# A feed-forward's second projection as 2x2 blocks in seven products

## The chip, the cores and the metric

The kernel runs on one core of a Trainium2 chip. The metric is the device time of one execution in microseconds; 2852.32 is the median of three runs (2851.64 to 2853.88). The engines are named as the profile names them: PE is TensorE (PEld its weight loads), DVE VectorE, ACT ScalarE, POOL GpSimd, SP SyncE.

## What is computed

One transformer block of two layers (attention mixers, then a feed-forward with a convolution) and a second block with a plain gated feed-forward, a mixer and a feed-forward again, on 512 tokens of width 1024 in float32: seven stages m0, f0, m1, f1, s0, m2, s1, of which four (f0, f1, s0, s1) are feed-forwards. Only these change:

```python
def conv_ffn(h, w_up, conv_w, conv_b, w_down):          # f0, f1
    u = h @ w_up                                        # 1024 -> 2 x 2816
    u = lax.conv_general_dilated(u, conv_w[:, None, :], ...) + conv_b   # over 3 tokens, per channel
    gate, up = jnp.split(u, 2, axis=-1)
    return (jax.nn.gelu(gate, approximate=True) * up) @ w_down          # 2816 -> 1024

def _swiglu(x, w_gate, w_up, w_down):                   # s0, s1
    return (jax.nn.silu(x @ w_gate) * (x @ w_up)) @ w_down
```

What comes out is normed, scaled by a gain and added to the residual x; the next stage begins with a norm of x.

## The kernel before

Every float32 operand of a matmul is split in two: hi, a rounded copy that ScalarE makes, and lo, the rest, a subtraction on VectorE. A product is three matmuls (hi·hi, hi·lo, lo·hi, `mm3`, lines 220 to 225).

`Weights` (line 30) is the planner. SyncE loads chunks of up to 1 MB into two raw buffers (`_load`, line 89). A chunk holds units of 1024 columns per partition, and `_split` (line 103) writes a unit's hi and lo into one of four slots; the last unit's rest also issues the load of the chunk after the next (line 122). `get` takes the next unit, `done` frees a slot and splits ahead as far as slots go. `lend` adds slots for a few units. Every engine runs its instructions in the order in which the program writes them, so a split that waits for a load holds what is behind it on ScalarE.

A feed-forward (`ffn`, line 603) runs in two parts of 11 k-tiles (a k-tile: 128 of the 2816 inner channels). For each pair of k-tiles `gemm_T` computes two gate and two up tiles (128 channels x 512 tokens, 24 matmuls each); `post_g` and `post_u` turn them into the product g, and `split2` (line 227) writes it into `gh`, `gl`. Behind the 11 k-tiles follows the second projection with `out_part` (line 520): output half h (512 columns), four token tiles of 128, stationary `gh[:, k, tokens]`, moving the weight unit. The first part's result goes into `part`; the second part's (`out_last`, line 553) is added, squared on ScalarE for the norm, and multiplied by the gain (half 0 on VectorE, half 1 on GpSimd). The last four units run token tile by token tile, and `finish` (line 575) makes a token tile's new x and, through `pre_norm` (line 329), its normed row hn, which `turn` (line 371) transposes on TensorE and `evacuate` splits for the next stage. From there on rests of weights are made on GpSimd (`W.lo`), ahead for the next stage.

Of the kernel before, what the change touches and what calls it, by code (L numbers as in the profile page):

```python
# [16 lines left out]
T = 512  # L17
# [11 lines left out]

class Weights:  # L30
# [6 lines left out]
    def __init__(self, nc, pool):  # L37
# [6 lines left out]
        self.units = []  # L44
        self.loaded = 0
# [25 lines left out]
    def add(self, srcs, a, b, unit_slices):  # L71
        c = len(self.chunks)
        self.chunks.append((srcs, a, b))
        for n, (a0, a1, b0, b1) in enumerate(unit_slices):
            self.units.append((c, a0, a1, b0, b1, n == len(unit_slices) - 1))
# [27 lines left out]
    def _split(self):  # L103
        u = self.split
        c, a0, a1, b0, b1, last = self.units[u]
        _, a, b = self.chunks[c]
        if c >= self.loaded:
            self.flush()
        raw = self.raw[c % self.NRAW][:, :a * b].rearrange("p (a b) -> p a b", a=a)[:, a0:a1, b0:b1]
# [3 lines left out]
        self.late.append((lo, raw, hi, c + self.NRAW if last else 0))  # L113
# [4 lines left out]
    def flush(self):  # L118

        for lo, raw, hi, nxt in self.late:  # L120
            self.lo.tensor_sub(lo, raw, hi.bitcast(F32))  # L121
            self._load(nxt)
        self.late = []

    def ahead(self, keep=1):

        self.flush()
        while self.split < len(self.units):
# [8 lines left out]
    def view(self, u):  # L137
        _, a0, a1, b0, b1, _ = self.units[u]
        n = (a1 - a0) * (b1 - b0)
        return tuple(t[:, :n].rearrange("p (a b) -> p a b", a=a1 - a0) for t in self.where[u])  # L140
# [33 lines left out]
class Net:  # L174
# [418 lines left out]
    def reg_ffn(self, wg, wg0, wu, wu0, wd):  # L593
        W = self.W
        for k0, nk in ((0, 11), (11, 11)):
            for j in range(k0, k0 + nk, 2):
                m = min(2, k0 + nk - j)
                W.cols(wg, wg0 + j * 128, m * 128)
                W.cols(wu, wu0 + j * 128, m * 128)
            for h in range(2):  # L600
                W.rows(wd, k0, nk, h * 512, 512)

    def ffn(self, conv, half, last, gpost, gpre_next):
# [3 lines left out]
        with ExitStack() as st:  # L607
            P = st.enter_context(self.tc.tile_pool(name="ffn", bufs=1))
            gh = P.tile([128, 11, T], F32R, name="gh")
            gl = P.tile([128, 11, T], F32R, name="gl")  # L610
            part = P.tile([128, 4, D], F32, name="part")
            tmp = ExitStack()
            Q = tmp.enter_context(self.tc.tile_pool(name="ffntmp", bufs=1))
            cg = [Q.tile([128, T], F32, name=f"cg{i}") for i in range(3)]
            gg = [Q.tile([128, T], F32, name=f"gg{i}") for i in range(2)]
            if conv is not None:
                cu = [Q.tile([128, T], F32, name=f"cu{i}") for i in range(3)]
                cw = Q.tile([128, 2 * NFT, 4], F32, name="cw")
                nc.gpsimd.dma_start(cw, conv)

# [15 lines left out]
            def post_u(j, jj):  # L636
                def f(ps):
                    g = gg[j % 2]
                    if conv is not None:
# [4 lines left out]
                    self.split2(gh[:, jj], gl[:, jj], g)  # L644
# [5 lines left out]
            for p in range(2):  # L650
                k0 = p * 11
                for jj in range(0, 11, 2):
                    m = min(2, 11 - jj)
                    posts = [post_g(k0 + jj + e) for e in range(m)] + [post_u(k0 + jj + e, jj + e) for e in range(m)]
# [6 lines left out]
                if p == 0:  # L661
                    for h in range(2):
                        def post0(i, ps):
                            if i % 2:
                                nc.vector.tensor_copy(part[:, i, h * 512:h * 512 + 512], ps)
                            else:
                                nc.scalar.activation(part[:, i, h * 512:h * 512 + 512], ps, AF.Copy)
                        self.out_part((gh, gl), 11, post0)
                else:
# [1084 lines left out]
```

## Time and profile before

| | us |
|---|---|
| median of the runs | 2852.32 |
| profiled execution: its own time | 2851.37 |
| profiled execution: span from first to last instruction | 2849.4 |
| TensorE busy | 2790.2 |
| VectorE busy | 1397.4 |
| ScalarE busy | 1102.0 |
| GpSimd busy | 365.3 |

Busy time of TensorE counts pipelined records that overlap, so its share says that it hardly ever waits, not that it runs at its peak; what one matmul costs is the distance from start to start.

### The profile page before, as it was taken

How to read it: one execution, taken by the hardware profiler on the slowest of the kernel's cores; microseconds unless marked ns; L12 is line 12 of the kernel's file. 1: busy time of each engine (PE TensorE's matmuls, PEld its weight loads, DVE VectorE, ACT ScalarE, POOL GpSimd, SP SyncE). 2: the span in 40 equal slices, each digit the busy share in tenths (PEclk: the TensorE clock that was granted, in tenths of full speed). 3: DMA queues.
4: the chain of work that ended last, by engine and by line, in shares of the span. 5: the costliest groups of instructions: out<-in, count | busy, mean ns of one | idle time of the engine just before them, and what ended most of it. 6: DMA issues, size and time to landing. Idle time of an engine off the chain costs nothing.

```text
span 2849.4 us, 34641 instructions
## 1 busy us (share of the span) xinstructions
PE 2790.2 (98%) x14196; PEld 2282.4 (80%) x14196; DVE 1397.4 (49%) x2126; ACT 1102.0 (39%) x1886; POOL 365.3 (13%) x285
## 2 busy tenths in 40 slices
PE   8999999999999999999999999999999999999998
PEld 7778688888878787788888888888777978888887
DVE  4666645535555666455535453233653343533334
ACT  3444634423444456444334332223343322432232
POOL 5221100100122221000101110000522000000000
PEclk9999999999999999999999999999999999999999
DMA  4211132333322111233332323323421223322332
GB/s 148 74 57 34 34 130 86 105 115 108 111 71 91 60 38 45 82 119 95 108 103 91 110 89 100 100 81 118 140 74 53 72 78 97 111 94 92 104 97 73
DMA packets 234318, 255.45 MB, mean 90 GB/s; under 512 B 33072, under 2 KB 193184, under 8 KB 233776
## 3 DMA queue, kind: packets, MB, share of 16 engines
q1 hardware_dynamic: 228016, 233.53, 25.7%
q0 software_dynamic: 4992, 16.94, 1.9%
q8 instruction: 111, 1.82, 0.3%
q10 hardware_dynamic: 1152, 2.77, 0.3%
q14 instruction: 47, 0.39, 0.0%
HBM read 248.60 MB, written 5.53 MB: 89 GB/s over the span
## 4 chain that ended last, share of the span: by engine, by line
PE 90%; DVE 5%; ACT 3%; issue 1%; DMA 0%; DVEq 0%; ACTq 0%; POOL 0%; POOLq 0%
PE PS L223 26%; PE PS L225 25%; PE PS L224 25%; PE PS L422 2%; DVE x L585 2%; PE PS L1124 1%; PE PS L1110 1%; PE PS L1080 1%; PE PS L425 1%; PE PS L460 1%; DVE hn L339 1%; PE PS L1220 1%; PE PS L1192 1%; PE PS L380 1%; PE PS L1511 1%
## 5 line engine op out<-in xcount | busy, mean ns | idle before, releaser
L121 DVE TENSOR_TENSOR wlo<-wraw,whi 128x1024 fp32r<-128x1024 f32 (+3 forms) x366 | 440.3, 1208 | 726.5 <-ACT whi L112 726.4
L223 PE MATMUL PS<-Hh,whi 128*128 128x512 f32 x1952 | 776.1, 398 | 4.1 <-DVE oBl L232 2.8
L225 PE MATMUL PS<-Hh,wlo 128*128 128x512 f32 x1952 | 761.0, 390 | 0.9 <-DVE wlo L121 0.9
L224 PE MATMUL PS<-Hl,whi 128*128 128x512 f32 x1952 | 760.6, 390 | 0.0
L112 ACT ACTIVATE whi<-wraw 128x1024 fp32r<-128x1024 f32 (+2 forms) x432 | 436.9, 1016 | 340.0 <-PE PS L225 279.5
L223 PEld LDWEIGHTS PS<-Hh,whi 128*128 128x128 f32 x1952 | 366.5, 188 | 88.3 <-issue 8.7
L225 PEld LDWEIGHTS PS<-Hh,wlo 128*128 128x128 f32 x1952 | 366.4, 188 | 79.2 <-DVE wlo L121 1.5
L224 PEld LDWEIGHTS PS<-Hl,whi 128*128 128x128 f32 x1952 | 367.0, 188 | 70.5
L121 POOL TENSOR_TENSOR wlo<-wraw,whi 128x1024 fp32r<-128x1024 f32 (+1 forms) x66 | 162.8, 2467 | 1268.1 <-ACT whi L112 1268.1
L223 PE MATMUL PS<-whi,gh 128*128 128x512 f32 x624 | 242.8, 389 | 0.0
L224 PE MATMUL PS<-wlo,gh 128*128 128x512 f32 x624 | 242.7, 389 | 0.0
L225 PE MATMUL PS<-whi,gl 128*128 128x512 f32 x624 | 242.7, 389 | 0.0
L231 ACT ACTIVATE gh<-gg 128x512 fp32r<-128x512 f32 x88 | 55.7, 632 | 327.2 <-DVE gg L643 178.9
L223 PEld LDWEIGHTS PS<-whi,gh 128*128 128x128 f32 x624 | 117.3, 188 | 24.3
L225 PEld LDWEIGHTS PS<-whi,gl 128*128 128x128 f32 x624 | 117.1, 188 | 24.4
L224 PEld LDWEIGHTS PS<-wlo,gh 128*128 128x128 f32 x624 | 117.1, 188 | 24.4
L641 POOL TENSOR_TENSOR gg<-cg,cu 128x512 f32<-128x512 f32 x44 | 56.7, 1289 | 549.4 <-DVE cu L624 549.4
L232 DVE TENSOR_TENSOR gl<-gg,gh 128x512 fp32r<-128x512 f32 x88 | 60.9, 693 | 125.6 <-ACT gh L231 125.6
L223 PE MATMUL PS<-whi,Hh 128*128 128x512 f32 (+2 forms) x320 | 118.2, 369 | 1.9 <-ACT whi L112 1.6
L224 PE MATMUL PS<-wlo,Hh 128*128 128x512 f32 (+2 forms) x320 | 116.7, 365 | 0.5 <-DVE wlo L121 0.5
L225 PE MATMUL PS<-whi,Hl 128*128 128x512 f32 (+2 forms) x320 | 116.5, 364 | 0.0
L1091 DVE TENSOR_REDUCE small<-PS 128x2 f32<-128x256 f32 (+3 forms) x64 | 52.7, 824 | 72.0 <-PE PS L1082 61.2
(355 smaller groups left out, 3966.0 us busy)
## 6 DMA issues: line engine op xcount, KB each, us to landing
wraw<-in_w_in_dram SPq DMA_DIRECT2D x56, 1024.0 KB, 5.0
wraw<-in_w_up_dram SPq DMA_DIRECT2D x40, 1024.0 KB, 5.1
wraw<-in_ffn_w_gate_dram SPq DMA_DIRECT2D x20, 1024.0 KB, 5.2
wraw<-in_ffn_w_up_dram SPq DMA_DIRECT2D x20, 1024.0 KB, 5.3
wraw<-in_w_down_dram SPq DMA_DIRECT2D x16, 1024.0 KB, 5.0
wraw<-in_ffn_w_down_dram SPq DMA_DIRECT2D x16, 1024.0 KB, 5.0
wraw<-in_w_out_dram SPq DMA_DIRECT2D x12, 1024.0 KB, 4.9
wraw<-in_w_down_dram SPq DMA_DIRECT2D x8, 768.0 KB, 4.3
```

Source lines behind the costliest of these rows:

```text
L112: self.nc.scalar.activation(hi, raw, AF.Copy)
L121: self.lo.tensor_sub(lo, raw, hi.bitcast(F32))
L223: mm(out, lh, rh, start=start, stop=False)
L224: mm(out, lh, rl, start=False, stop=False)
L225: mm(out, ll, rh, start=False, stop=stop)
L231: nc.scalar.activation(hi, src, AF.Copy)
L232: nc.vector.tensor_sub(lo, src, hi.bitcast(F32))
L339: nc.vector.scalar_tensor_tensor(hn, self.x[:, i], r, self.gpre, op0=OP.mult, op1=OP.mult)
L422: self.nc.tensor.matmul(ps[:, sl], ww[:, k], self.Hh[:, k, sl], start=k == 0 and ww is w[0], stop=False)
L585: nc.vector.scalar_tensor_tensor(x, f, r, x, op0=OP.mult, op1=OP.add)
L641: nc.gpsimd.tensor_mul(g, cg[j % 3], cu[j % 3])
L1091: nc.vector.reduce_max(m, S2, axis=AX.X, negate=True)
```

## The change

The second projection of each part becomes a product of 2x2 blocks. Even and odd k-tiles of the part are the two blocks of the inner dimension, tokens 0 to 255 and 256 to 511 the two of the rows, the output halves the two of the columns. Seven products of sums of blocks, added into the four output blocks with signs, replace the eight plain ones. A feed-forward has three parts (6, 8 and 8 k-tiles, so P = 3, 4, 4 pairs).

`post_u` makes the sums of activation blocks with four VectorE operations for every pair of k-tiles and splits seven operands of 256 tokens (`Ah`, `Al`). `Weights.quad` lists the weight units in the order of the products: the raw buffers hold two blocks (x and y), a third (z) is loaded by SyncE into free rows, and the sums are made in place, by accumulating transfers from GpSimd's queue, each issued when the unit that it overwrites has been split. `down` runs the seven products ("steps"), keeps three pairs of PSUM banks of which two are accumulated into more than once, and adds each output into `part` with its sign. In the last part (`fin`) it also squares, multiplies by the gain (both halves on VectorE), queues `finish`, and splits the next stage's units; three operands' places are lent as slots. `out_part` and `out_last` stay for the other stages. The core of the diff:

```diff
@@ -72,7 +78,45 @@
+    def quad(self, w, k0, P):
+        v = w.rearrange("(k p) n -> p k n", p=128)
+        block = lambda o, h: v[:, k0 + o:k0 + 2 * P:2, h * 512:h * 512 + 512]
+        b12, b21, b22 = block(0, 1), block(1, 0), block(1, 1)
+        c, q = len(self.chunks), Quad()
+        self.chunks += [([(0, 128, b)], P, 512) for b in (b22, block(0, 0))]
+        q.block, q.P = b21, P
+        part = [slice(i, min(i + 2, P)) for i in range(0, P, 2)]
+        y = lambda i: self.raw_of(c)[:, part[i]]
+        x = lambda i: self.raw_of(c + 1)[:, part[i]]
+        z = lambda i: q.room[i][:, :part[i].stop - part[i].start]
+        plus = lambda t, b: lambda i: self.nc.gpsimd.dma_start(t(i), b[:, part[i]], accum_op=OP.add)
+        load = lambda c: lambda i: self._load(c) if i == len(part) - 1 else None
+        for src, after in ((x, plus(x, b12)), (x, plus(x, b22)), (y, plus(y, b12)), (z, None), (x, plus(x, b21)),
+                           (y, load(c + 2)), (x, load(c + 3))):
+            for i, s in enumerate(part):
+                self.units.append((c + 1, lambda i=i, src=src: src(i), s.stop - s.start, 512,
+                                   [lambda i=i, f=after: f(i)] if after else []))
+        self.quads.append(q)
+    def open_quad(self, room):
+        q = self.quads.pop(0)
+        q.room = room
+        for i in range(0, q.P, 2):
+            m = min(2, q.P - i)
+            self.nc.sync.dma_start(room[i // 2][:, :m], q.block[:, i:i + m])
+        return q.P
...
     def flush(self):
-        for lo, raw, hi, nxt in self.late:
+        late, self.late = self.late, []
+        for lo, raw, hi, after in late:
             self.lo.tensor_sub(lo, raw, hi.bitcast(F32))
-            self._load(nxt)
-        self.late = []
-    def ahead(self, keep=1):
+            for f in after:
+                f()
+    def ahead(self, keep=1, upto=1 << 30):
...
     def reg_ffn(self, wg, wg0, wu, wu0, wd):
         W = self.W
-        for k0, nk in ((0, 11), (11, 11)):
+        for k0, nk in self.PARTS:
             for j in range(k0, k0 + nk, 2):
-                m = min(2, k0 + nk - j)
-                W.cols(wg, wg0 + j * 128, m * 128)
-                W.cols(wu, wu0 + j * 128, m * 128)
-            for h in range(2):
-                W.rows(wd, k0, nk, h * 512, 512)
+                W.cols(wg, wg0 + j * 128, 256)
+                W.cols(wu, wu0 + j * 128, 256)
+            W.quad(wd, k0, nk // 2)
+    PARTS = ((0, 6), (6, 8), (14, 8))
+    def down(self, Ah, Al, room, part, first, fin=None):
+        nc, W = self.nc, self.W
+        u0 = W.taken
+        if fin:
+            self.normed = 0
+            W.lend([tuple(t[:, op].rearrange("p m t -> p (m t)") for t in (Ah, Al)) for op in (0, 3, 6)], 10)
+        P = W.open_quad(room)
+        nu = (P + 1) // 2
+        a, b, c = [[self.bank(), self.bank()] for _ in range(3)]
+        steps = ((0, a, False, 0, 0, 1, True, False), (3, b, False, 1, 1, -1, True, False), (6, b, True, 0, 1, -1, True, False),
+                 (1, c, False, 0, 0, 1, False, True), (4, a, True, 0, 1, -1, False, True), (5, a, True, 1, 1, -1, False, True),
+                 (2, a, True, 1, 0, 1, True, True))
+        for n, (op, banks, on, row, h, sign, new, end) in enumerate(steps):
+            ws = [W.get() for _ in range(nu)]
+            if fin:
+                if n == 2:
+                    self.table(SQRT_SET)
+                W.ahead(0, u0 + nu * (n + (3 if n == 3 else 2)))
+                if n == 5:
+                    W.defer, W.lo = True, nc.gpsimd
+                    W.ahead(0)
+            else:
+                W.ahead(0)
+            for e in range(2):
+                i, ps = 2 * row + e, banks[e]
+                tok = slice(e * 128, e * 128 + 128)
+                for m in range(P):
+                    lhs = Ah[:, op, m, tok], Al[:, op, m, tok]
+                    w = ws[m // 2]
+                    for x, (l, r) in enumerate(((0, 0), (0, 1), (1, 0))):
+                        nc.tensor.matmul(ps, lhs[l], w[r][:, m % 2], start=not on and m + x == 0, stop=m == P - 1 and x == 2,
+                                         skip_group_check=on)
+                    if fin and n == 6 and e == 1 and m == P // 2 - 1:
+                        self.bi += 2
+                        self.turn(1)
+                        self.evacuate()
+                if e == 1:
+                    W.free_only(nu)
+                f = part[:, i, h * 512:h * 512 + 512]
+                if new and first:
+                    if e:
+                        nc.vector.tensor_scalar(f, ps, float(sign), None, op0=OP.mult)
+                    else:
+                        nc.scalar.activation(f, ps, AF.Copy, scale=float(sign))
+                elif sign > 0:
+                    nc.vector.tensor_add(f, ps, f)
+                else:
+                    nc.vector.tensor_sub(f, f, ps)
+                if fin:
+                    if n == 6 and e == 0:
+                        self.turn(0)
+                    if end:
+                        fin(i, h, c[e] if n in (4, 5) else ps)
+                    self.pump()
+                    self.evacuate()
+                    W.flush()
+        if fin:
+            self.pump()
+            W.ahead(0)
+            W.flush()
+            W.defer, W.lo = False, nc.vector
+            W.give_back()
...
-            gh = P.tile([128, 11, T], F32R, name="gh")
...
+            Ah = P.tile([128, 7, 4, 256], F32R, name="Ah")
+            Al = P.tile([128, 7, 4, 256], F32R, name="Al")
...
+            S = [h.rearrange("p (s t) -> p s t", s=4) for h in self.hn]
...
-                    self.split2(gh[:, jj], gl[:, jj], g)
+                    m, s = jj // 2, S[jj // 2 % 2]
+                    (g11, g21), (g12, g22) = [[t[:, h * 256:h * 256 + 256] for h in range(2)] for t in gg]
+                    if jj % 2 == 0:
+                        late.append(lambda: self.split2(Ah[:, 0, m], Al[:, 0, m], g11))
+                    else:
+                        nc.vector.tensor_sub(s[:, 0], g22, g21)
+                        nc.vector.scalar_tensor_tensor(s[:, 1], s[:, 0], -1.0, g11, op0=OP.mult, op1=OP.subtract)
+                        nc.vector.tensor_sub(s[:, 2], g11, g21)
+                        nc.vector.scalar_tensor_tensor(s[:, 3], g12, -1.0, s[:, 1], op0=OP.mult, op1=OP.subtract)
+                        late.append(lambda: self.split2(Ah[:, 1:3, m], Al[:, 1:3, m], g.rearrange("p (h t) -> p h t", h=2)))
+                        late.append(lambda: self.split2(Ah[:, 3:7, m], Al[:, 3:7, m], s))
...
+                run_late()
+                e = (k0 + nk - 2) % 3
+                room = [tm[:, 2 * i:2 * i + 2] for i in ((e + 2) % 3, e, (e + 1) % 3, 3)]
+                def fin(i, h, sq):
+                    f = part[:, i, h * 512:h * 512 + 512]
+                    nc.scalar.activation(sq, f, AF.Square, accum_out=sst[:, h * 4 + i:h * 4 + i + 1])
+                    nc.vector.tensor_mul(f, f, self.gpost[:, h * 512:h * 512 + 512])
+                    if h == (i < 2):
+                        self.side.append(self.finish(i, part[:, i, :512], part[:, i, 512:], sst[:, i:i + 1],
+                                                     sst[:, 4 + i:5 + i], half, last))
+                self.down(Ah, Al, room, part, p == 0, fin if k0 + nk == NFT else None)
+            while self.side:
+                self.pump()
```

## Rows read from the trace of the kernel before

**Rows 1.** The page of the whole span: its head, busy share per engine, TensorE's clock

```profile
span 2849.4 us, 34641 instructions
...
PE 2790.2 (98%) x14196; PEld 2282.4 (80%) x14196; DVE 1397.4 (49%) x2126; ACT 1102.0 (39%) x1886; POOL 365.3 (13%) x285
...
PEclk9999999999999999999999999999999999999999
```

**Rows 2.** Timeline of TensorE, first and last of 117: start us, length us, instruction

```profile
559.71 0.39 PE L225 MATMUL PS<-Hh,wlo 128*128 128x512 f32 x1
...
586.01 0.39 PE L224 MATMUL PS<-Hl,whi 128*128 128x512 f32 x1
```

**Rows 3.** Groups of TensorE in 559.9 to 586.05 us; one of three alike

```profile
L223 PE MATMUL PS<-Hh,whi 128*128 128x512 f32 x39 | 15.2, 389 | 0.0
```

**Rows 4.** Groups, whole span: second projections' first term (count, busy us, mean ns, idle)

```profile
L223 PE MATMUL PS<-whi,gh 128*128 128x512 f32 x624 | 242.8, 389 | 0.0
...
L223 PE MATMUL PS<-mhi,gh 128*128 128x512 f32 x80 | 32.8, 410 | 0.0
```

**Rows 5.** Timeline of TensorE, waiting instructions at feed-forwards' ends: [idle before <- what ended it]

```profile
823.12 1.44 PE L380 MATMUL PS<-cf,hn 128*128 128x128 f32 x8 [1.90 <-DVE small L580]
...
830.86 1.07 PE L380 MATMUL PS<-cf,hn 128*128 128x128 f32 x8 [0.30 <-DVE small L580]
...
846.53 0.50 PE L460 MATMUL PS<-whi,Hh 128*128 128x512 f32 x1 [0.80 <-ACT Hh L231]
...
1649.02 0.38 PE L422 MATMUL PS<-Hh,whi 128*128 128x256 f32 x1 [1.10 <-ACT Hh L231]
...
2024.07 0.50 PE L460 MATMUL PS<-wlo,Hh 128*128 128x512 f32 x1 [1.48 <-POOL wlo L121]
```

**Rows 6.** Groups by shape, whole span: splits of weights, and the norm (count, busy, mean ns)

```profile
L121 DVE TENSOR_TENSOR wlo<-wraw,whi 128x1024 fp32r<-128x1024 f32 x327 | 411.2, 1262 | 658.0 <-ACT whi L112 657.9
L112 ACT ACTIVATE whi<-wraw 128x1024 fp32r<-128x1024 f32 x392 | 410.2, 1050 | 281.7 <-PE PS L225 235.4 <-issue 18.9 <-DMA wraw<-in_w_up_dram 9.4
L121 POOL TENSOR_TENSOR wlo<-wraw,whi 128x1024 fp32r<-128x1024 f32 x65 | 161.0, 2477 | 1256.2 <-ACT whi L112 1256.2
...
L339 DVE SCALAR_TENSOR_TENSOR hn<-x,small,gpre 128x1024 f32<-128x1024 f32 x28 | 38.6, 1380 | 4.6 <-DMA gpre<-in_g_pre_mix_dram 3.6
```

**Rows 7.** DMA issues: queue, count, KB each, median us from issue to landing

```profile
wraw<-in_w_down_dram SPq DMA_DIRECT2D x16, 1024.0 KB, 5.0
...
wraw<-in_w_down_dram SPq DMA_DIRECT2D x8, 768.0 KB, 4.3
...
nab<-na_bias POOLq DMA_DIRECT2D x3, 1024.0 KB, 10.3
...
gpost<-in_g_post_ffn_dram POOLq DMA_DIRECT2D x2, 512.0 KB, 3.9
```

**Rows 8.** Timelines of ScalarE and GpSimd behind one `up` tile, first feed-forward

```profile
578.67 0.76 ACT L622 ACTIVATE cu<-PS,cw 128x512 f32<-128x512 f32 x1
...
581.63 1.29 POOL L641 TENSOR_TENSOR gg<-cg,cu 128x512 f32<-128x512 f32 x1 [4.49 <-DVE cu L624]
```

**Rows 9.** Timeline of VectorE at the first feed-forward's end

```profile
800.53 0.68 DVE L672 TENSOR_TENSOR part<-PS,part 128x512 f32<-128x512 f32 x1
...
802.61 0.68 DVE L672 TENSOR_TENSOR part<-PS,part 128x512 f32<-128x512 f32 x1
...
815.79 4.16 DVE L585 SCALAR_TENSOR_TENSOR x<-part,small,x 128x512 f32<-128x512 f32 x2
```

**Rows 10.** Timeline of GpSimd at the same end

```profile
816.56 2.85 POOL L121 TENSOR_TENSOR wlo<-wraw,whi 128x1024 fp32r<-128x1024 f32 x1
```

**Rows 11.** Timeline of all engines at the end of the span

```profile
2844.16 1.99 DVE L585 SCALAR_TENSOR_TENSOR x<-part,small,x 128x512 f32<-128x512 f32 x2
```

**Rows 12.** Windows: length, busy us (instructions) per engine, TensorE's granted clock, DMA share, GB/s

```profile
823.70:827.10 3.40, 3.40 (x12) 2.81 (x11) 3.40 (x2) 0.00 (x0) 3.40 (x2) 0.50 0.01 4
...
2008.10:2011.50 3.40, 3.40 (x10) 2.63 (x9) 3.40 (x2) 0.00 (x0) 2.88 (x2) 0.50 0.00 0
```

More of the change, by code (lines that the diff above doesn't have):

```diff
@@ L27, with __init__ @@
 PI = 3.141592653589793
+class Quad:
+    def __init__(self):
+        self.room = None
 class Weights:
@@ L44, in __init__ @@
         self.units = []
+        self.quads = []
         self.loaded = 0
@@ L104, in _split @@
         u = self.split
-        c, a0, a1, b0, b1, last = self.units[u]
-        _, a, b = self.chunks[c]
-        if c >= self.loaded:
+        c, src, _, _, after = self.units[u]
+        if self.late and (c >= self.loaded or len(self.late) > 1):
             self.flush()
-        raw = self.raw[c % self.NRAW][:, :a * b].rearrange("p (a b) -> p a b", a=a)[:, a0:a1, b0:b1]
+        raw = src()
         self.where[u] = (self.extra if self.extra and self.first <= u < self.limit else self.free).pop(0)
@@ L112, in _split @@
         self.nc.scalar.activation(hi, raw, AF.Copy)
-        self.late.append((lo, raw, hi, c + self.NRAW if last else 0))
+        self.late.append((lo, raw, hi, after))
         self.split += 1
@@ L118, in flush @@
     def flush(self):
-        for lo, raw, hi, nxt in self.late:
+        late, self.late = self.late, []
+        for lo, raw, hi, after in late:
             self.lo.tensor_sub(lo, raw, hi.bitcast(F32))
-            self._load(nxt)
-        self.late = []
-    def ahead(self, keep=1):
+            for f in after:
+                f()
+    def ahead(self, keep=1, upto=1 << 30):
         self.flush()
-        while self.split < len(self.units):
+        while self.split < min(upto, len(self.units)):
             extra = self.extra and self.first <= self.split < self.limit
@@ L137, in view @@
     def view(self, u):
-        _, a0, a1, b0, b1, _ = self.units[u]
-        n = (a1 - a0) * (b1 - b0)
-        return tuple(t[:, :n].rearrange("p (a b) -> p a b", a=a1 - a0) for t in self.where[u])
+        _, _, a, b, _ = self.units[u]
+        return tuple(t[:, :a * b].rearrange("p (a b) -> p a b", a=a) for t in self.where[u])
     def get(self):
@@ L649, in ffn @@
             sst = self.sm(8)
[L650 to L654, printed above, removed]
+            for p, (k0, nk) in enumerate(self.PARTS):
+                for jj in range(0, nk, 2):
+                    posts = [post_g(k0 + jj + e) for e in range(2)] + [post_u(k0 + jj + e, jj + e) for e in range(2)]
                     if p == 0 and jj == 0:
@@ L660, in ffn @@
                         self.gemm_T(f, soon=True)
[L661 to L669, printed above, removed]
-                    def post1(i, ps, h):
-                        f = part[:, i, h * 512:h * 512 + 512]
-                        nc.vector.tensor_add(f, ps, f)
-                        nc.scalar.activation(ps, f, AF.Square, accum_out=sst[:, h * 4 + i:h * 4 + i + 1])
-                        (nc.gpsimd if h else nc.vector).tensor_mul(f, f, self.gpost[:, h * 512:h * 512 + 512])
-                    tmp.close()
-                    with self.tc.tile_pool(name="more", bufs=1) as M:
-                        self.W.lend(self.W.slots(M, 3, "m"), 9)
-                        self.out_last((gh, gl), 11, lambda i, ps: post1(i, ps, 0), lambda i, ps: post1(i, ps, 1),
-                                      lambda i: self.finish(i, part[:, i, :512], part[:, i, 512:], sst[:, i:i + 1],
-                                                            sst[:, 4 + i:5 + i], half, last))
-                        self.W.give_back()
-                    while self.side:
-                        self.pump()
+                run_late()
+                e = (k0 + nk - 2) % 3
[10 more added lines that the diff above has]
+                self.pump()
     def proj(self, nk, mov, post):
```

23 lines of the change are left out of this document (15 added, 8 removed).

## The prediction

> **What bounds the kernel now.** Read the page's busy line and clock line first: TensorE works through 98% of the span at the full 2.4 GHz clock [rows 1]. Any matmul taken out is therefore worth its issue interval, as long as nothing else begins to make TensorE wait. That interval comes from the timeline: from 559.71 to 586.01 us stand 117 matmuls (three terms of 39), so 26.30 / 116 = 0.227 us each [rows 2, 3]; the 0.39 of one record is its pipelined length. Then read the second projections: 624 + 80 stationary tiles for each of three terms, 2112 matmuls in all four feed-forwards, 528 in one [rows 4]. Last, read where TensorE does wait in and behind a feed-forward: nowhere inside, only at its end, when transposes of the next stage's input wait for the norm, and the next stage for its first weights or tokens. There are four waits like 1.90, two like 0.30, two like 1.48, one of 1.10 and one of 0.80, together 13.1 us [rows 5].
>
> **What is removed.** Per feed-forward 11 pairs of k-tiles, 7 products, 2 token tiles and 3 terms make 462 matmuls in place of 528. Four times 66 are 264 matmuls, 264 x 0.227 = **59.8 us gained**, if nothing else gets late. A product ("step") of 4 k-tile pairs is 24 matmuls or 5.44 us, one of 3 is 4.08.
>
> **Work added beside TensorE.** Weight blocks to split rise from 44 to 77 per feed-forward (of 128x512 each), 16.5 more splits of 1024 columns at 1.05 us on ScalarE and 1.26 on VectorE [rows 6]; per step that is two of each, about 3.5 us with their start, inside 5.44 or (one and a half) 4.08. The activations' sums are four VectorE operations of 256 columns and a split of 7x256 columns in place of 4x256 per pair of tiles, some 3 us more in 21.8 us of matmuls. Inside the first projection I cost both at nothing, since VectorE is busy half of the span [rows 1]; without that cover they would be 3 us for each of 44 pairs. The z loads and the sums' extra bytes (SyncE and GpSimd queues) also go beside matmuls, at nothing.
>
> **The accumulating transfers.** No row shows one. Nearest is a plain 512 KB transfer from GpSimd's queue: 3.9 us from issue to landing; three of 1 MB queued together take 10.3 in the median [rows 7]. Lower bound 3.9, upper 10.3. I take 5.5: it is nearest to the plain row, and the destination must be read too, which I price as another 512 KB at the difference between a 1 MB and a 768 KB load on SyncE's queue (0.7 per 256 KB) [rows 7]. What covers them: step 0's first unit is split about 6 us before step 0 starts (x arrives 5.0 after the last `up` unit is split, and then 1.05 and 1.26 pass), and step 1's first unit must be copied by ScalarE when step 0 starts. So 5.5 just fits, and every microsecond above about 6 holds ScalarE, with the copies queued behind it. The other sums have a step or more in between. The Trainium skill (DMA: Bandwidth & Descriptors, Anatomy of one DMA) fits 2.0 us plus bytes over 436 GB/s to a transfer from that queue: 3.2 us for 512 KB, where the row has 3.9. By it a second pass over the bytes would land at 4.4, under 6 like my 5.5, so the sum is the same and only the rival below gets less likely; no run here shows it.
>
> **Step 1 of each quad in the two feed-forwards with a convolution.** After the last first-projection tile the product of gate and up is there at 581.63 + 1.29 - 578.67 = 4.25 us [rows 8]. Then come four sums of 256 columns (half of a 0.68 us operation with its start, 0.4 each: 5.85), ScalarE's copy of the 1024 summed columns (6.9), VectorE's rest (8.15), and only then the rest of step 1's second weight unit, which stands behind them in VectorE's queue: 9.3. TensorE wants it after step 0 and six matmuls, at 5.44 + 1.36 = 6.8: it waits 2.5 us, twice; in the quad of 3 it wants it at 5.44, and the unit has half the columns: 3.4. That is 8.4 per feed-forward and **17 us** for the two. Without a convolution the product is there some 3.5 us earlier, and nothing waits. Before, the last tiles' splits were needed only by the last of 11 k-tiles. Bounds: 0 (if 256-column sums and splits are shorter) and 25.
>
> **The last quad of each feed-forward.** Here I expect most of the loss, because VectorE now does everything in order while matmuls grow fewer. From step 3's start its queue holds: the wait for ScalarE's first copy 1.05; four weight rests 4.8; four cycles of add, Square on ScalarE, multiply by gpost, 2.08 each from 800.53 to 802.61, 8.3 [rows 9]; for tokens 0 and 1 bias, root, reciprocal and two updates of x, about 2.2 each with a Square between; the rests of step 6's two units 2.4; and the subtraction that frees the bank which step 6 accumulates into, 0.7. Together 22 us, against three steps of 16.3: **5.7 us late**, in all four. Second, at step 5 the loader also copies the next stage's third unit. Its chunk is loaded only when step 6's units are split: 21.3 + 5.0 after step 3's start, and ScalarE waits for it in order. Behind it stand the Square of token 2, then the multiply (next to GpSimd's 2.48 us rest, which holds it as 815.79's two updates were held to 4.16 us by 816.56's [rows 9, 10]) and hn of token 0 (1.38 [rows 6]): 32 us. The transposes of token 0 stand in TensorE's queue after half of step 6, at 24.7: **7.3 us**, three times (the last feed-forward has no next stage). Third, the next stage's fourth weight unit is split behind everything that tokens 2 and 3 still ask of ScalarE, about 10 us after the last matmul, plus GpSimd's 2.48; a mixer asks for it after 4.5 us: **8.7 us** for two mixers, and about 4 for the feed-forward that follows one and wants token 1's transposes. Last, at the kernel's end the chain behind the last matmul (its updates of x begin at 2844.16, and a store follows [rows 11]) grows by a queued cycle, 2 us. Sum: 4 x 5.7 + 3 x 7.3 + 2 x 8.7 + 4 + 2 = 68, less the 13 of today that they replace: **55 us**. Bounds: 20, if the loaded chunk holds nobody, and 65.
>
> **Clock.** After the 1.90 us wait at 823.12 the granted clock was 0.50 for 3.4 us [rows 5, 12]: 1.7 us lost. Two of the three ends show it [rows 12]. Waits of 5 to 8 us should bring it at least twice in each of three ends: some **6 us** more; bounds 0 and 15.
>
> **Sum.** -59.8 + 17 + 55 + 6 = +18 us. The profiled execution took 2851.4 us with a span of 2849.4 [rows 1]; the median of the runs is 2852.3, 0.9 above it. I predict 2852.3 + 18 = **2870 us**.
>
> **Rivals.** (A) Accumulating transfers are slow. It decides from 6 us on (8 without convolution). At 8 us each quad with a convolution loses 2 more, the one of 3 k-tile pairs 3.4 (its sum between steps 4 and 6 is late too), the others 2 in the small quad only: 2 x 7.4 + 2 x 2 = 19, 2889 us; at 10 us some 51, 2921. For it: an addition reads two streams. Against: 3.9 for the plain one. Chance 0.18. (B) Faster: the chunk for the next stage's third unit lands before ScalarE reaches its copy. Place: step 5 of the last quad. It decides if the load leaves 5 us earlier than I have it. Then the 7.3 goes three times, the fourth unit comes 5 us sooner at two mixers, and 4 us of the slow clock go: 22 + 10 + 4 = 36, and the first-projection tail with less queued may give some more: 2830 us. For it: VectorE is only half busy on the page. Against: that share is a mean, and this stage's queue is full. Chance 0.2. (C) The clock falls at the quads as well. The waits of step 1 come in two pieces of a microsecond, with a matmul between; six quads at 1.7 us are 10 us: 2880. The Trainium skill (TensorE: Matmul & The Clock Gate, HAM oscillation) has a loop that waits at every tile go cold each time; this trace shows waits of 1.9 us both with and without a fall, so neither is excluded. Chance 0.08. (D) Little of each, gains and losses even out within 0.2% (5.7 us, about what a measurement of this kernel can tell from no change): chance 0.12. My forecast: 0.42.
>
> **How the numbers follow.** Slower by over 0.2%: 0.42 + 0.18 + 0.08 = 0.68; within: 0.12; faster: 0.2. The range has to reach into A and B: down to the first by B's 2830 with a little less won, 2834, up to an accumulation between 8 and 10 us, 2905. Slower outcomes alone would be 2858 to 2905.
>
> **What would show it.** The second projection's groups count 1848 matmuls at an unchanged 0.39 us. In every convolution quad TensorE waits two times at step 1's third k-tile, first for ScalarE's, then for VectorE's part of the weights. In the last quad it waits for a VectorE subtraction before step 6, and for hn before token 0's transposes, while ScalarE waits for a load. The accumulating transfers land in 5 to 6 us. I am wrong if they take over 8, if the ends of the feed-forwards cost TensorE no more than today's 13 us, or if VectorE falls behind inside the first projection.

## The result and the profile after

The changed kernel takes 2897.2 us (median of 4 runs, 2895.6 to 2899.3) beside 2852.0 for the kernel before on the same chip: 45 us or 1.6% slower (ratio 1.016, 95% interval 1.0143 to 1.0178). The forecast was +18. The profiled executions have spans of 2897.5 and 2849.4 us.

The page of the changed kernel: its span, the busy lines of TensorE, VectorE, ScalarE and GpSimd, and the granted clock in 40 slices, to be held against [rows 1].

```profile
span 2897.5 us, 35039 instructions
...
PE 2770.3 (96%) x13932; PEld 2254.7 (78%) x13932; DVE 1616.6 (56%) x2538; ACT 1206.4 (42%) x2002; POOL 464.7 (16%) x365
...
PEclk9999999999989999999999999999899999999999
```

TensorE is busy 96% of the span, and two slices fall below 90% of full clock (a 9 stands for 90% or more). The mean granted clock of the whole span, with the kernel before first:

```profile
core 0: 2849.4 us, clock 0.995
```

```profile
core 0: 2897.5 us, clock 0.979
```

The second projection's groups (page; out<-in, shapes, count, busy us, mean ns, idle before) count 3 x 568 and three small groups of 48 that read borrowed buffers, 1848 in all. That answers [rows 4]: the 264 matmuls are gone.

```profile
L681 PE MATMUL PS<-whi,Ah 128*128 128x512 f32 x568 | 228.4, 402 | 17.6 <-ACT Ah L274 9.9
L681 PE MATMUL PS<-wlo,Ah 128*128 128x512 f32 x568 | 228.0, 401 | 5.4 <-DVE wlo L165 5.4
L681 PE MATMUL PS<-whi,Al 128*128 128x512 f32 x568 | 227.2, 400 | 1.7 <-DVE Al L275 1.7
```

The mean of one is 400 to 402 ns, against 389 before [rows 4]: a first sign of the clock. The list of what TensorE waits for (total us, times, longest us; L423 is a transpose, L681 the second projection, L503 a mixer's first projection):

```profile
PE PS L423 <- DVE hn L382: 20.9, 5, 5.5
PE PS L681 <- DVE part L698: 19.7, 8, 5.1
PE PS L681 <- ACT Ah L274: 9.9, 2, 5.5
PE PS L503 <- ACT whi L155: 8.5, 2, 5.7
PE PS L681 <- ACT whi L155: 7.6, 5, 1.9
PE PS L681 <- DVE wlo L165: 5.4, 6, 1.0
PE PS L423 <- DVE small L623: 5.1, 6, 1.5
```

**Where the 48 us of span went.** From the start of every TensorE matmul in the trace I took the interval to the next. What exceeds the usual interval of the same form by over 0.3 us is a wait; what exceeds it by less, inside a stretch with a granted clock of 0.50, is slow clock. (Usual interval: the mean over all traces of this study, waits left out; summed over a kernel it runs a few us high, which is the last column. Of an interval that waits inside a slow stretch, up to one usual interval is counted as slow clock and the rest as a wait.) In us, for the runs that the argument needs:

| kernel | all intervals | at usual interval | waits | slow clock | rest |
|---|---|---|---|---|---|
| before | 2839.1 | 2777.6 | 60.9 | 10.2 | -9.6 |
| changed | 2885.0 | 2716.0 | 131.1 | 46.1 | -8.3 |
| run e1_busy | 2875.9 | 2766.1 | 95.4 | 21.9 | -7.4 |
| run e5_last_plain | 2828.3 | 2738.3 | 80.2 | 17.8 | -7.9 |
| run e7_s_quads | 2815.6 | 2758.4 | 58.4 | 8.3 | -9.4 |

Before to changed: -61.6 for the matmuls, +70.2 of waits, **+35.9 of slow clock**, +1.3 of rest, and 2.2 more behind the last matmul. The forecast had -59.8, +72 (of which 2 behind the last matmul) and +6. So matmuls and waits were sized right in sum, and the clock was not. For the waits the sum is luck: those of the quads (a quad is one second projection of a part, seven steps) came out 11 us above their term and those of the ends 11 below theirs. Where the line between the last two columns is drawn matters too: if an interval that waits in a slow stretch is counted wholly as a wait, the changes are +77 of waits and +28 of slow clock. Their sum stays within 2 us, and 28 is still far above 6.

**What a stretch at half clock looks like.** Windows of the changed kernel (length, busy us and count of PE, PEld, DVE, ACT, POOL, granted clock, DMA share, GB/s): the first behind step 0's wait in the first quad, the second behind step 1's in the second quad, the third inside a feed-forward without a convolution.

```profile
540.10:546.90 6.80, 5.96 (x13) 4.29 (x14) 4.81 (x9) 2.30 (x5) 2.47 (x2) 0.50 0.57 114
669.80:676.60 6.80, 5.98 (x14) 4.45 (x14) 5.20 (x7) 2.04 (x3) 3.63 (x3) 0.50 0.52 88
1763.00:2004.00 241.00, 241.00 (x1065) 199.54 (x1064) 122.68 (x156) 85.47 (x104) 18.32 (x16) 1.00 0.48 128
```

The level of 0.50 (1.2 of 2.4 GHz) holds in 18 such stretches from the first feed-forward to the end of the last, 99 us together; [rows 12] show the two that there were in the same part before, 6.8 us together. They last 3.4 to 10.2 us. Where TensorE did not wait, the clock was 1.00 for 241 us.

### The profile page after: what moved, and what is told of

It reads as the page before. It is cut to its first block, busy times and chain, and to the rows that moved or that the text cites. A ratio compares the mean times of both kernels' runs of the same rounds, so it can differ in the third digit from the quotient of the medians.

```text
span 2897.5 us, 35039 instructions
## 1 busy us (share of the span) xinstructions
PE 2770.3 (96%) x13932; PEld 2254.7 (78%) x13932; DVE 1616.6 (56%) x2538; ACT 1206.4 (42%) x2002; POOL 464.7 (16%) x365
## 4 chain that ended last, share of the span: by engine, by line
PE 44%; DVE 4%; ACT 2%; issue 2%; DMA 2%; POOL 0%; DVEq 0%; ACTq 0%; POOLq 0%
PE PS L266 11%; PE PS L268 10%; PE PS L267 10%; PE PS L681 8%; DMA wraw<-in_w_down_dram 1%; PE PS L465 1%; DVE wlo L165 1%; PE PS L503 1%; PE PS L1630 1%; PE PS L468 0%; ACT PS L795 0%; DVE x L628 0%; DVE part L796 0%; DVE Al L165 0%; ACT whi L155 0%
## 5 line engine op out<-in xcount | busy, mean ns | idle before, releaser
L165 DVE TENSOR_TENSOR wlo<-wraw,whi 128x1024 fp32r<-128x1024 f32 (+2 forms) x414 | 484.3, 1184 | 493.6 <-ACT whi L155 493.3
L155 ACT ACTIVATE whi<-wraw 128x1024 fp32r<-128x1024 f32 (+3 forms) x480 | 479.9, 1010 | 424.1 <-PE PS L681 99.8
L681 PE MATMUL PS<-whi,Ah 128*128 128x512 f32 x568 | 228.4, 402 | 17.6 <-ACT Ah L274 9.9
L681 PE MATMUL PS<-wlo,Ah 128*128 128x512 f32 x568 | 228.0, 401 | 5.4 <-DVE wlo L165 5.4
L681 PE MATMUL PS<-whi,Al 128*128 128x512 f32 x568 | 227.2, 400 | 1.7 <-DVE Al L275 1.7
L103 POOL DMA_DIRECT2D wraw<-in_ffn_w_down_dram x48 | 55.4, 1192 | 592.7 <-DVE wlo L165 582.0
L681 PEld LDWEIGHTS PS<-whi,Ah 128*128 128x128 f32 x568 | 110.1, 194 | 44.4 <-ACT Ah L274 11.3
L681 PEld LDWEIGHTS PS<-wlo,Ah 128*128 128x128 f32 x568 | 110.3, 194 | 30.6 <-DVE wlo L165 7.4
L681 PEld LDWEIGHTS PS<-whi,Al 128*128 128x128 f32 x568 | 110.3, 194 | 27.7 <-DVE Al L275 4.5
L760 POOL TENSOR_TENSOR tm<-tm 128x512 f32<-128x512 f32 x44 | 69.6, 1581 | 384.8 <-DVE tm L741 383.8
```

Of the source, the lines that this page charges most:

```text
L103: plus = lambda t, b: lambda i: self.nc.gpsimd.dma_start(t(i), b[:, part[i]], accum_op=OP.add)
L155: self.nc.scalar.activation(hi, raw, AF.Copy)
L681: nc.tensor.matmul(ps, lhs[l], w[r][:, m % 2], start=not on and m + x == 0, stop=m == P - 1 and x == 2, skip_group_check=on)
L760: nc.gpsimd.tensor_mul(g, cg[j % 3], cu[j % 3])
```

## Experiments

Each run was measured beside the kernel before on its own chip (medians 2853.7 us for e1 to e4, 2852.4 for e5 to e8, 2851.7 for e9 to e11); the ratios are to that. The code cuts are shortened, and `...` marks what is left out.

**e1: work in the waits.**

```diff
+    def busy(self, n, ps):
+        for _ in range(n):
+            self.nc.tensor.matmul(ps, self.Hh[:, 0, :128], self.Hh[:, 1, :], start=True, stop=True)
...
+                if fin and n == 6 and e == 0:
+                    self.busy(16, spare)
...
+                    if conv and e == 0 and m == 2 and (n == 1 or n == 0 and first):
+                        self.busy(10 if n else 20, c[0])
...
+                            self.busy(18, self.PS[:, self.banks[self.bi % 8], :])
```

> TensorE gets matmuls whose results nobody reads, only where the changed kernel waits: 20 ahead of the third k-tile of step 0 of the small quad and 10 ahead of that of step 1 in every quad (both only with a convolution), 16 ahead of step 6 and 18 ahead of token 0's transposes in each last quad. Between the two kernels the waits grew by 69 us (forecast 72), but matmuls issued at the half clock cost 41 us instead of 10. Theory 1, the granted clock falls because TensorE stands still in these waits, and this is a loss of its own beside the waits: most of the half-clock stretches behind these waits go (13 of 19), and the time falls by 10 to 20 us, to 2877 to 2887. Theory 2, the clock falls whatever TensorE does in a wait, or what it gives back is waited for later: 2895 to 2905, since the filling can only delay the work behind it.

2890.9 us (ratio 1.0135, 1.012 to 1.015): 6 us less, between the theories. The table shows why: the slow clock falls by 24 us, so it does come from TensorE standing still; but the matmuls put in take 50 and the waits fall by only 36. Work at full clock reaches the next wait sooner, and that one ends when VectorE or a load is done, not earlier. After the filling ahead of token 0's transposes, intervals of 3.3 to 3.7 us remained: from the last matmul of the product to the transposes it is 7.3 to 7.7 us, beside 5.3 to 6.1 in the changed kernel. The mean granted clock rises from 0.979 to 0.990:

```profile
core 0: 2888.8 us, clock 0.990
```

So the clock's 36 us are no loss that could be had back whole: of 24 recovered, 9 of the intervals' sum and 6 of the time stayed.

**e2: transfers that replace instead of adding.**

```diff
- self.nc.gpsimd.dma_start(t(i), b[:, part[i]], accum_op=OP.add)
+ self.nc.gpsimd.dma_start(t(i), b[:, part[i]])
```

> The transfers that add a weight block onto the one in the buffer only replace it: same bytes from memory, same order, same waits, but nothing is added (the sums of weight blocks are left out of the computation). Theory 1, in the small quad of the two feed-forwards with a convolution ScalarE is held by the accumulating transfer (4.6 us until 539.45), and with it the copy that step 0's third k-tile waits for: a plain 512 KB transfer lands in about 4 us instead of 6, so the wait of 5.9 and 4.8 us there falls to about 3, the steps 1 behind it gain up to 1 us, and the time falls by 4 to 8 us to 2889 to 2893. Theory 2, the addition costs nothing and 6 us are what the queue needs for any transfer in this place: landing stays at 6 us and the time at 2895 to 2899.

2891.8 us (ratio 1.0132, 1.0116 to 1.0147, just overlapping the changed kernel's interval). The DMA issues (queue, count, KB each, median us from issue to landing), first the changed kernel's two, then e2's:

```profile
wraw<-in_w_down_dram POOLq DMA_DIRECT2D x40, 512.0 KB, 6.1
wraw<-in_ffn_w_down_dram POOLq DMA_DIRECT2D x40, 512.0 KB, 5.8
```

```profile
wraw<-in_w_down_dram POOLq DMA_DIRECT2D x40, 512.0 KB, 4.3
wraw<-in_ffn_w_down_dram POOLq DMA_DIRECT2D x40, 512.0 KB, 4.2
```

And the wait for ScalarE's `Ah` in e2's list of waits:

```profile
PE PS L681 <- ACT Ah L274: 5.9, 2, 3.1
```

Adding costs 1.6 to 1.8 us of landing time, and without it the two waits fall from 9.9 to 5.9. Theory 1 fits, with some 5 us of the 45 (8 by the ratios).

**e3: only two units of the next stage at step 5.**

```diff
-                    W.ahead(0)
+                    W.ahead(0, u0 + nu * 7 + 2)
...
+                    if n == 6 and e == 0:
+                        W.ahead(0, u0 + nu * 7 + 3)
```

> At step 5 of the last quad the loader copies only two units of the next stage; the third, whose chunk is still being loaded, is copied after the first half of step 6. Theory 1 (the prediction's second point on the last quad), ScalarE is held by that load (5.1 us from 834.7 on), and only so token 0's transposes wait 5.9, 5.2 and 5.6 us: these three waits fall under 1 us, with them the half-clock stretches behind them (some 3 us each), and the time falls by 16 to 26 us to 2871 to 2881. Theory 2, VectorE's queue would make the transposes wait as long, or the third unit is missed by the next stage instead: 2890 to 2899.

2885.1 us (ratio 1.0112, 1.0097 to 1.0127), 12 less. The wait for `hn`, 20.9 us in 5 with a longest of 5.5, becomes

```profile
PE PS L423 <- DVE hn L382: 13.0, 10, 3.3
...
PE PS L503 <- ACT whi L155: 7.1, 2, 4.3
```

The 5 us waits ahead of token 0 are gone (intervals of 1.5, 1.2 and 1.7 are left), so the held ScalarE was their cause. Most of it is waited for again, at token 1 (1.4 twice, new) and at the next stage's first weights: all waits of the account fall by 5 us only, and slow clock by 11. Theory 1 for the cause; the size lies between the two ranges.

**e4 and e9: the quads of the feed-forwards with a convolution.** e4 takes the fourth product second and issues the last sums later:

```diff
+            steps = (steps[0], steps[3], steps[1], steps[2]) + steps[4:]
...
+            if n == 0 and sums is not None:
+                sums[0]()
```

> In the first two quads of the two feed-forwards with a convolution the fourth product (block loaded on its own, activations that are no sums) comes second, its block's load is issued one tile of the first projection earlier, and the four sums of the last pair of tiles and their split are issued behind the split of this product's weights. Theory 1, step 1 waits because sums and their split stand ahead of the weights' rest in VectorE's queue, and in the small quad also because ScalarE is held by the accumulating transfer: the waits of these four quads (7.1, 3.7, 7.5 and 3.9 us) and the half clock there (2.8, 2.8, 1.5 and 1.7) go, 31 us: 2863 to 2873. Theory 2, they only move one step on (the sums are now late for the third product) or the block loaded on its own lands too late for step 1: 2885 to 2897.

2902.2 us (ratio 1.0174, 1.0157 to 1.0191): 5 us more than the changed kernel with overlapping intervals, so nothing is gained; theory 2, and above its range. e9 also issues the weights of the second and third step ahead of the last splits (its cut against e4's; `n = 0` issues the split of the last product, `n = 1` the four sums and theirs):

```diff
-                if early:
-                    late.pop(0)()
...
+            if n < 2 and sums is not None:
+                sums[0][n]()
```

> As the run with the fourth product second (2902), with the in-order queues rearranged: at the quad's start the weights of its second step are split before the last pair's products are, and the four sums and their split are issued at the start of the second step, behind the weights of the third. Theory 1, the steps behind the first waited because on ScalarE copies of weights stood behind a copy that waited for the last product on GpSimd (3.1 us) or for the sums (2.8 us), and on VectorE their rests behind the sums; the sums themselves are in time. Then the waits of the second quads go and those of the small ones shrink to the 4 us for the product of the last tile but one: of 31 us of waits and half clock some 10 are left, 2897 - 21 = 2876, within 2870 to 2884. Theory 2, the product itself comes too late (convolution, gate and GpSimd in a chain), whatever the order behind it: 2890 to 2902.

2891.8 us (ratio 1.0142, 1.0127 to 1.0157), 5 less than the changed kernel: inside theory 2's range. In its second quad 2.3 us of waits are left of 3.8, in the small one (3 pairs) 6.2 of 7.3, both in the first feed-forward. What remains is the chain to the product itself. ScalarE of e9 (start us, duration, line, out<-in, idle before and what ended it):

```profile
660.86 0.42 ACT L277 ACTIVATE Ah<-tm 128x256 fp32r<-128x256 f32 x1 [3.40 <-POOL tm L767]
661.18 0.77 ACT L746 ACTIVATE tm<-PS,cw 128x512 f32<-128x512 f32 x1
664.97 1.06 ACT L158 ACTIVATE whi<-tm 128x1024 fp32r<-128x1024 f32 x1 [3.02 <-DMA tm<-in_w_down_dram]
```

ScalarE waits 3.4 us for GpSimd's product of one tile before it begins the convolution of the next (L746), which the product and sums of that tile follow.

**e5, e6, e7: which feed-forward, and which part of it.** e5 does the last 8 k-tiles of every feed-forward in the former way (8 block products, `out_last`); e6 keeps the former feed-forward (`ffn_old`) in the two with a convolution; e7 does both.

```diff
-                self.down(Ah, Al, room, part, p == 0, fin if k0 + nk == NFT else None)
+                if k0 + nk < NFT:
...
+                    self.down(Ah, Al, room, part, p == 0)
+                    continue
...
+                    (nc.gpsimd if h else nc.vector).tensor_mul(f, f, self.gpost[:, h * 512:h * 512 + 512])
...
+                self.out_last((gh, gl), nk, lambda i, ps: post1(i, ps, 0), lambda i, ps: post1(i, ps, 1),
...
-                self.ffn(a["conv"][l], False, nxt is None, a["g_post_ffn"][l], pre[nxt])
+                self.ffn_old(a["conv"][l], False, nxt is None, a["g_post_ffn"][l], pre[nxt])
```

> The first two quads of every feed-forward keep their 7 products; the last 8 k-tiles are done as in the kernel before (8 block products, token by token, with its way of finishing). That puts back 4 x 24 matmuls x 0.227 = 21.8 us. Theory 1 (the prediction's largest term): the ends are slow because of the 7-product order there. Waits and half clock in the four ends of the changed kernel are 31, 22, 28 and 9 us, of which some 9 are step 1 and 13 to 16 were there before the change, so about 64 go: 2897 + 22 - 64 = 2855, within 2848 to 2862. Theory 2, the ends wait for something that the change put elsewhere (memory shared with the product's buffers, the queues' backlog out of the quads before): less than half of it goes, 2885 or more.

2840.0 us (ratio 0.9959, 0.9944 to 0.9974): 57 us less than the changed kernel, though 96 matmuls came back, and 15 less than expected. Waits fall by 51 and slow clock by 28 in the table. So the way in which the last quads were done is the cause of the slow ends. Which part of that way is not shown: the former way also goes token by token and puts half 1's multiply by gpost back on GpSimd, and no run separates these from the number of products.

> The two feed-forwards with a convolution are those of the kernel before; the two without are those of the changed kernel. By the traces the changed kernel loses 29 and 14 us from one feed-forward's start to the next one's in the first two, and 9 less 6 in the others. Theory 1, they are independent: 2852 + 3 = 2855, within 2851 to 2859, so the convolution's feed-forwards carry nearly the whole loss of 45. Theory 2, the loss is one of the chip's state over the whole kernel (clock, memory): it falls in proportion, about 2875.

2854.0 us (ratio 1.0006, 0.9996 to 1.0015): theory 1. The feed-forwards are independent, and the two with a convolution carry 43 of the 45 us.

> 7 products only where the changed kernel showed no wait: the first two quads of the two feed-forwards without a convolution; all else as in the kernel before. 2 x 7 pairs of k-tiles x 6 matmuls = 84 matmuls less, x 0.227 = 19 us. Theory 1, the product's saving is real wherever its sums are hidden: 2852 - 19 = 2833, within 2830 to 2839. Theory 2, the added splits, sums and transfers cost something even there, or the change of way from the quads to the last 8 k-tiles does: 2840 to 2855.

2828.3 us (ratio 0.9919, 0.9902 to 0.9936): **24 us faster than the kernel before** and the best kernel here. Its page (engines, granted clock) has TensorE busy 98% and no slice below 90% of full clock:

```profile
PE 2768.5 (98%) x14112; PEld 2265.6 (80%) x14112; DVE 1474.8 (52%) x2262; ACT 1136.1 (40%) x1924; POOL 396.6 (14%) x315
...
PEclk9999999999999999999999999999999999999999
```

The largest line of its waits is of the kind and length that [rows 5] begin with:

```profile
PE PS L423 <- DVE small L623: 12.3, 11, 1.9
```

The 84 matmuls are worth 19 us; 2.5 less waits and 1.9 less slow clock account for most of the rest.

**e8: step 6's weights split in the middle of step 4.**

```diff
+                    if n == 4 and e == 0:
+                        W.ahead(0, u0 + nu * 7)
```

> The changed kernel with one thing moved: in each last quad step 6's weight units are split in the middle of step 4, not at the start of step 5. So VectorE's two rests (2.4 us) no longer stand ahead of the subtraction that step 6 waits for, and the load of the chunk with the next stage's third unit leaves about 7 us earlier. Theory 1 (the prediction's first and second point on the last quad): the waits of 4.3, 4.3, 4.3 and 5.5 us ahead of step 6 fall to about 2, those of 5.9, 5.2 and 5.6 us ahead of token 0's transposes fall under 2, some half-clock stretches go, and part of it comes back at the next stage's fourth unit: 20 to 30 us less, 2867 to 2877. Theory 2, step 4 now waits instead (the sum for step 6 lands late, so ScalarE is held a step earlier, or VectorE's rests are late for step 5): 2885 or more.

2885.9 us (ratio 1.0118, 1.0103 to 1.0134), 11 less, at the edge of theory 2's range. In step 5 a wait of 3.4 us stands in place of the 1.1 and 4.3 of steps 5 and 6 (three ends; 5.0 in the last), and ScalarE is no longer held by the load. The same copy, and `hn` of token 0, in the timelines of the changed kernel and of e8:

```profile
839.84 1.06 ACT L155 ACTIVATE whi<-wraw 128x1024 fp32r<-128x1024 f32 x1 [5.12 <-PE PS L681]
...
843.97 1.28 DVE L382 SCALAR_TENSOR_TENSOR hn<-x,small,gpre 128x1024 f32<-128x1024 f32 x1
```

```profile
834.01 9.05 POOL L165 TENSOR_TENSOR wlo<-wraw,whi 128x1024 fp32r<-128x1024 f32 x3 [15.30 <-ACT whi L155]
...
835.07 1.06 ACT L155 ACTIVATE whi<-wraw 128x1024 fp32r<-128x1024 f32 x1 [0.20 <-DMA wraw<-in_w_in_dram]
...
837.58 3.23 DVE L382 SCALAR_TENSOR_TENSOR hn<-x,small,gpre 128x1024 f32<-128x1024 f32 x1
...
841.44 0.60 ACT L797 ACTIVATE PS<-part 128x512 f32<-128x512 f32 x1 [3.33 <-DVE part L698]
```

(In the first the page names TensorE, which was done long before; the load was issued at 834.87.) But here token 0's transposes still wait 2.0 us and token 1's 2.1, and in the next two ends token 0's wait 5.2 and 2.9: `hn` takes 3.2 us in all three, beside GpSimd's rests, where it took 1.28 without them, and each Square waits for VectorE's subtraction. With the load out of the way, VectorE's serial cycles, stretched beside GpSimd, are the bound.

**e10, e11: can the convolution's quads pay?** e10 is e5 with the order of e9; e11 cuts the k-tiles 8, 8, 6.

```diff
-    PARTS = ((0, 6), (6, 8), (14, 8))
...
+    PARTS = ((0, 8), (8, 8), (16, 6))
```

> The order of the run just described in the first two quads of the feed-forwards with a convolution, and the last 8 k-tiles of every feed-forward as in the kernel before (that alone took 2840). Theory 1: the same 21 us less, 2819, within 2813 to 2828, and so faster than 7 products in the feed-forwards without a convolution alone (2828). Theory 2: 2835 to 2845.

> As the last one, with the k-tiles cut 8, 8 and 6 (the last 6 as in the kernel before) in place of 6, 8 and 8. No quad of three pairs is left, in which step 0 wants the last pair's product 2.7 us after it starts, not 4.1; and 8 of 11 pairs go by 7 products, not 7. Theory 1: 4 x 6 matmuls x 0.227 = 5.4 less and in the two first quads some 3 us less each: 2819 - 11 = 2808, within 2802 to 2816. Theory 2, six k-tiles at the end (a half of three weight units) are too short to cover the norms and the next stage's first weights: 2818 to 2835.

2837.1 us (ratio 0.9949, 0.9932 to 0.9965) and 2853.3 us (1.0003, 0.9994 to 1.0013). e10 lies in theory 2's range; e11 lies 18 us above both of its ranges. So in the orders tried the convolution's quads do not pay: e10, which has them, takes 9 us more than e7, which has not. In e11 the first quads still wait 3.8 us for `Ah` with four pairs, and the shorter ends no longer cover the norm; the wait that was 1.9 in [rows 5] is up to 7.2:

```profile
PE PS L426 <- DVE small L626: 20.6, 9, 7.2
PE PS L692 <- ACT Ah L277: 7.6, 4, 3.4
...
PE PS L506 <- DVE Hl L278: 5.9, 1, 5.9
```

## Why the prediction was right or wrong, step by step

**The sign and the mechanisms were right; the step that failed is the clock, +6 us with bounds 0 and 15, which measured +36.** It priced a wait of 5 to 8 us like the fall after the 1.90 us wait [rows 5, 12]: one stretch of 3.4 us, two in each of three ends. The traces show stretches of up to 10.2 us, three, two and four of them in those ends and one in the last feed-forward's, and one at the waits of each convolution quad as well. By place: some 20 us in the four ends (3 before), 12 in the six quads with a convolution, some 4 in attention stages whose waits did not change. Rival C had the second of these in kind and size (10 us) with a chance of 0.08, but left the ends at 6. The Trainium skill (TensorE: Matmul & The Clock Gate, HAM oscillation) says that a loop that waits at each tile goes cold each time; the six quads here agree, each with one stretch of 3.4 or 6.8 us at 0.50 at its waits. e1 shows that the falls go when TensorE is kept busy (46 to 22), and also that this returns 6 us only: the term is real in the account of the trace, but most of it lies ahead of waits that other engines set. So in the account the 27 us between forecast and result (30 by the spans) are this term, and their cure is fewer waits: e5 and e7 lose waits and slow clock together.

**Removed matmuls, 59.8.** Right: 264 fewer, 61.6 at the usual interval of all traces.

**Added work beside TensorE at nothing.** Right where the product is early: 241 us without a wait in the window above, and e7 gains its full 19. The sums and splits cost nothing inside the first projection.

**Accumulating transfers, 5.5 taken.** They land in 5.8 to 6.1 us, and GpSimd's instruction takes 1.19 where e2's plain one takes 0.69:

```profile
L103 POOL DMA_DIRECT2D wraw<-in_ffn_w_down_dram x48 | 55.4, 1192 | 592.7 <-DVE wlo L165 582.0
```

At 6.1 in the feed-forwards with a convolution that is just past the point of 6 us from which rival A decides, and in the small quads it did, as forecast: ScalarE is held by the transfer, and the copies queue behind it. Its size there is e2's 5 us. The Trainium skill (DMA: Bandwidth & Descriptors, Anatomy of one DMA) has a fit from which the prediction estimated 4.4 with a second pass over the bytes; here the measured 5.8 to 6.1 decide.

**Step 1 of the convolution's quads, 17 (0 to 25).** Too small: the six quads waited 28 us, above the bound. Step 1 itself behaved as told, first for ScalarE's and then for VectorE's part (7.6 in 5 and 5.4 in 6 in the list above; 15 us by intervals). What the step overlooked, and what makes the other 13 us, is step 0: it already wants the last pair's first tile after 1.4 us (3 pairs) or 2.0 (4 pairs), and in the first quad of each of these feed-forwards ScalarE was far behind. TensorE's timeline there, and ScalarE's:

```profile
533.82 0.39 PE L681 MATMUL PS<-whi,Ah 128*128 128x512 f32 x1
...
540.87 0.79 PE L681 MATMUL PS<-whi,Ah 128*128 128x512 f32 x1 [5.52 <-ACT Ah L274]
```

```profile
534.12 0.76 ACT L739 ACTIVATE tm<-PS,cw 128x512 f32<-128x512 f32 x1
539.45 1.06 ACT L155 ACTIVATE whi<-wraw 128x1024 fp32r<-128x1024 f32 x1 [4.57 <-DMA wraw<-in_w_down_dram]
540.41 0.40 ACT L274 ACTIVATE Ah<-tm 128x256 fp32r<-128x256 f32 x1
```

The quad starts at 533.82, but the convolution of the last `up` tile but one begins only at 534.12, though its matmuls were done a tile (5.4 us) before; then the transfer holds ScalarE for 4.57. In the second quad the same convolution begins at 655.34, 4.6 us ahead of the quad's first matmul. [Rows 8], on which the step rested, come from a place where ScalarE took up the tile within a microsecond of its end.

**The last quad, 55 (20 to 65).** 42 us more waits in the ends, and 2 behind the last matmul. By its points: late at steps 5 and 6, 5.7 four times: measured intervals of 1.1 and 4.3 (4.9 us of waiting in all) in three, 6.2 in the last. Token 0's transposes, 7.3 three times: 5.9, 5.1 and 5.6; e3 shows the load that holds ScalarE as the cause, e8 in two of the three ends. The fourth unit, 8.7 for two mixers: 5.5 and 8.4 in two pieces. The mechanisms stand at these places; each came out a little smaller in sum (for the fourth unit the prediction's own figures, 10 + 2.48 - 4.5, give 8.0), and the waits that they replaced were nearer 16 than 13. e3 and e8 show why removing one point pays only half: VectorE's cycles are close behind it.

**Rivals.** B (faster through an early load) falls as a kernel: even with the load out of the way (e8) the time stays 34 us above the kernel before. A and C were partly true, A at 5 us and C as 12 of the 36. D falls with the 45 us. None of the three signs of being wrong came: the transfers stay under 8, the ends wait more than before, and beyond its first tiles no first projection of a feed-forward makes TensorE wait by more than 0.3 us. None of them looked at the clock.

## What to carry to other kernels

A product scheme with fewer matmuls pays where its extra sums have a whole step of cover (e7, -24 us) and costs where the first steps want what was just produced or where a stage hands over. Price the end of a stage by the serial chain on the other engines, since fewer matmuls are also less cover for it. And when a change adds waits on TensorE, add the clock to them: here 70 us of waits brought 36 us of slow clock (77 and 28 by the other way of counting), though filling the waits gives only a small part of that back.

## What the runs showed of the hardware

An accumulating 512 KB transfer from GpSimd's queue lands 1.6 to 1.8 us later than a plain one in the same place (5.8 to 6.1 against 4.2 to 4.3), and its instruction holds GpSimd 0.5 us longer (1.19 against 0.69). Two waits of about 2.1 and 1.2 us with one matmul between them came with 6.8 us at half clock in the first feed-forward's second quad (669.80 to 676.60) and with 3.4 us in the quad after it: the wait's length alone did not tell how much slow clock there was. One operation of 1024 columns on VectorE (`hn`, which reads three operands) took 1.28 us with GpSimd idle and 3.2 beside GpSimd's subtractions (e8).
